# Weight sums of the seven-product units in another order, the first column released at the sixth product, and shared border transposes at the output

## Chip, cores and metric

The kernel runs on one core of a Trainium2 chip, in one launch. The metric is the device time of one execution in microseconds (us). Engines: PE is TensorE, with PEld its weight loads; DVE is VectorE, ACT ScalarE, POOL GpSimd and SP SyncE, which here mostly issues DMAs.

## What is computed

One streaming step of a hybrid layer for 512 prompt frames and 64 sample frames (576 frames, two halves of 288), all in fp32:

```python
hn = rmsnorm(x, g_norm1)
proj = hn @ w_in                                    # q, k, v | gb, gc, hc
q, k = rmsnorm(q, g_q), rmsnorm(k, g_k)
o_attn = stick_breaking_blocks(q, k_all, v_all, P)  # 8 heads x 128
u = gc * hc
conv = conv_w[0]*padded[:, 0:T] + conv_w[1]*padded[:, 1:T+1] + conv_w[2]*padded[:, 2:T+2]
o_conv = gb * conv                                  # 1024 channels
mix = concat([rmsnorm(o_attn, g_attn_out), rmsnorm(o_conv, g_conv_out)])
x = x + mix @ w_out
h2 = rmsnorm(x, g_norm2)
x = x + (silu(h2 @ w_gate) * (h2 @ w_up)) @ w_down
```

## The kernel before

An fp32 product is made of three fp32r matmuls: weights and frames are split into a high part (a CAST on ACT, then called the copy) and the rest (a TENSOR_TENSOR subtract on DVE, called the low part), and high x high, low x high and high x low are added up in PSUM.

Most large products are done in **units** of seven products in place of eight (Strassen-Winograd). A unit takes two weight columns of 128 (c = 0, 1), each cut by the parity of its input block: `a11`, `a12` lie in the first column, `a21`, `a22` in the second. The frames stand ready as 288-frame operands. Per unit four sums of 128 x 1024 weights are made on DVE. Before: at product 6 `s1 = a21 + a22`, `a21 = a21 - a11`, `a11 = s1 - a11`; at product 3 `a12 = a12 - a11`. Then products 1 to 7 use `a11, a12, a12', a22, s1, a11', a21'`. Products 1, 6, 5 and 3 add into one PSUM tile (`psy`), 7 and 4 into another (`psw`), 2 has its own (`psx`). ACT copies `psy` out (`part`) after products 1, 6 and 5, and DVE adds such parts to `psx` or `psw` (`cv`, in `done`).

The stages in order of time: attention heads and the first two convolution groups by plain products (line 214); `conv_run` (line 1012) with nine convolution units, numbers 0 to 8, and eight units 9 to 16 of the output projection's attention half, of 4 channel blocks in place of 8, whose frames (`forms`, seven of them, one per product) come back from DRAM; the other half of that projection by plain products; the first gate and up columns by plain products; gate and up units; down units (`run`, line 1526), whose results go out through `store_y` (line 1662).

For the convolution units, `corder` (line 1115) lists the products in their PE order as (unit, product). `conv_prepare` (line 968) makes the operand four places ahead: sums if due, the copy, the low part, into one of four `whl` buffers. PE's order is written out by hand. On ACT and DVE instructions stand in the order of the program only while `start_mode` is open (line 1128 on), else a scheduler places them; SP is in program order from unit 8 on (`turn_mode`).

Weight columns lie in three places: `raw_a` (two) and `raw_c`. `call_columns` (line 935) loads the next wanted column by an SP DMA as soon as one is free; a free place is announced by `conv_prepare`, the first column's at product 3, the second's at product 4. All SP DMAs go through one queue. At the start, columns (0,0), (0,1) and (1,0) (unit, column) are in place, and column (1,1) is the next. Just ahead of it SP issues the loads of the frame sums for products 4 and 5 of the convolution units: `xs_t` (line 862, 2304 KB) and eight loads of 288 KB into `x` (line 1112).

`store_y` turns a finished block of 128 columns x 288 frames by three PE transposes (128, 128 and 32 frames) into PSUM, copies 2 x 128 frames by one ACT copy and the 32 border frames by another (`obs`), and issues one DMA for the first half's 256 frames, three for the second half's, and one for each border. Each of eight down pairs d has four such blocks, (c, i) for column c and half i.

Of the kernel before, what the change touches and what calls it, by code (L numbers as in the profile page):

```python
# [20 lines left out]
HALF = T // 2  # L21
# [73 lines left out]
def tile_hybrid_stream_step(  # L95
# [6 lines left out]
    nc = tc.nc  # L102
# [119 lines left out]
    def split(hi, lo, src, lo_eng=None):  # L222
        nc.scalar.copy(out=hi, in_=src)  # L223
        (lo_eng or nc.vector).tensor_tensor(out=lo, in0=src, in1=hi.bitcast(F32), op=ALU.subtract)  # L224
# [259 lines left out]
    for i in range(5):  # L484
        n = P if i < 4 else TS
# [457 lines left out]
    def call_columns(gone):  # L943
        cfree.extend(gone)
        while cwanted:
            n, c = cwanted[0]
            place = [q for q in cfree if c is not None or q < 2][:1]
            if not place:
                return
            cwanted.pop(0)  # L950
            q = place[0]
            cfree.remove(q)
            raw = bt["raw"] if q == 2 else raw_tile["A"][:, q, :]
            if c is None:
                d = CU[n][1]
                nc.sync.dma_start(out=raw.rearrange("p (k c) -> p k c", c=2 * P),
                                  in_=w_out[:AW, 2 * d * P : 2 * (d + 1) * P].rearrange("(k p) c -> p k c", p=P))
                v = raw.rearrange("p (j s h c) -> p j s h c", s=2, h=2, c=P)
                for c in range(2):
                    cregion[n, c] = q, v[:, :, 0, c, :], v[:, :, 1, c, :]  # L960
            else:
                c0 = cstart[c + 2 * (CU[n][0] == "b")] + CU[n][1] * P
                nc.sync.dma_start(out=raw.rearrange("p (k c) -> p k c", c=P),
                                  in_=w_in[:, c0 : c0 + P].rearrange("(k p) c -> p k c", p=P))
                v = raw.rearrange("p (j s c) -> p j s c", s=2, c=P)
                cregion[n, c] = q, v[:, :, 0, :], v[:, :, 1, :]

    def conv_prepare(n, p_):
        st, tt, m = cst.setdefault(n, {"left": 7}), nc.vector.tensor_tensor, NP if n < NCU else NH // 2
        if p_ == 1:  # L970
            _, st["a11"], st["a12"] = cregion[n, 0]
        if p_ == 6:
            _, st["a21"], st["a22"] = cregion[n, 1]
            s1 = st["s1"] = bt["s1"][:, :m]
            tt(out=s1, in0=st["a21"], in1=st["a22"], op=ALU.add)
            tt(out=st["a21"], in0=st["a21"], in1=st["a11"], op=ALU.subtract)
            tt(out=st["a11"], in0=s1, in1=st["a11"], op=ALU.subtract)
        if p_ == 3:
            tt(out=st["a12"], in0=st["a12"], in1=st["a11"], op=ALU.subtract)
# [132 lines left out]
        nc.sync.dma_start(out=xt[j][:, 0, 1].bitcast(F32), in_=xs_dram[0, j].rearrange("f p t -> p f t"))  # L1112
    pipe.flush()
    open_units()
    corder = [(0, 1), (0, 2), (1, 1), (1, 2), (0, 6), (0, 7), (0, 5), (0, 3), (0, 4), (1, 6), (1, 7), (1, 5)]
    for n in range(2, len(CU)):
        if n == NCU - 1:
            corder += [(n, 1), (n - 1, 3), (n - 1, 4), (n, 6), (n, 7), (n, 5), (n, 2), (n, 4), (n, 3)]
        elif n == NCU:
            corder += [(n, 1), (n, 2), (n + 1, 1), (n + 1, 2), (n, 6), (n, 7), (n, 5), (n, 3), (n, 4)]  # L1120
            corder += [(n + 1, 6), (n + 1, 7), (n + 1, 5)]
        elif n == NCU + 1:
            pass
        else:
            corder += [(n, 1), (n - 1, 3), (n - 1, 4), (n, 2), (n, 6), (n, 7), (n, 5)]
# [478 lines left out]
    acc = {}  # L1604
    down = {}

    def take_blocks(d):

        if d in (0, 1, 3):
            spare_block({0: "z", 1: "t", 3: "ax"}[d])  # L1610
        if d in (0, 3):
            four = [down["z"][:, q, :] for q in (range(4) if d == 0 else range(4, 6))]
            if d:
                four += [down["ax"][:, q, :] for q in range(2)]
        elif d < 3:
            t = down["t"] if d == 1 else ypool.tile([P, 4, HALF], F32, tag=f"y{NP - 1}", name=f"acc{d}")
            four = [t[:, q, :] for q in range(4)]
        elif d < 6:
            four = [pool.tile([P, HALF], F32, tag=tag, name=f"acc{d}", bufs=2)
                    for pool, tag in (((tmp, "y"), (tmp, "r")) if d == 4 else ((tmp, "sq"), (h2pool, "hx")))  # L1620
                    for _ in range(2)]
        else:
            pool, tag = (tmp, "hl") if d == 6 else (rpool, "R")
            two = [pool.tile([P, 2, HALF], F32, tag=tag, name=f"acc{d}", bufs=2) for _ in range(2)]
            four = [t[:, q, :] for t in two for q in range(2)]
        for q, ap in enumerate(four):
            acc[d, q // 2, q % 2] = ap

    def spare_block(name):
        if name not in down:  # L1630
# [31 lines left out]
    def store_y(n, c, i):  # L1662

        d = UNITS[n][1]
        src, cs, f0 = acc[d, c, i], slice((2 * d + c) * P, (2 * d + c + 1) * P), HALVES[i][0]
        r = HALF - 2 * P

        def put(f, ap, q=nc.sync):

            rows, n_p = ap.shape[0], max(min(TP - f, ap.shape[0]), 0)  # L1670
            if n_p:
                q.dma_start(out=yp[f : f + n_p, cs], in_=ap[:n_p])
            if n_p < rows:
                q.dma_start(out=ys[f + n_p - TP : f + rows - TP, cs], in_=ap[n_p:])

        quick = n == NU - 1

        def work():
            yield 4 if quick else 9
            po = misc("pot")[:, : 3 * P]  # L1680
            for q in range(3):
                w = min(P, HALF - q * P)
                nc.tensor.transpose(po[:w, q * P : (q + 1) * P], src[:, q * P : q * P + w], ident)
            yield 0 if quick else 3
            ob = src[:, : 2 * P].rearrange("p (i c) -> p i c", c=P)
            nc.scalar.copy(out=ob, in_=po[:, : 2 * P].rearrange("p (i c) -> p i c", c=P))
            obs = down["pool"].tile([r, P], F32, tag="obs", name="obs", bufs=4)
            nc.scalar.copy(out=obs, in_=po[:r, 2 * P :])
            yield 0 if quick else 4
            if i == 0:  # L1690
                nc.sync.dma_start(out=yp[: 2 * P, cs].rearrange("(i p) c -> p i c", p=P), in_=ob)
            else:
                put(f0, ob[:, 0, :])
                put(f0 + P, ob[:, 1, :])
            put(f0 + 2 * P, obs, nc.scalar if quick else nc.sync)

        pipe.spawn(work())


# [76 lines left out]
```

## Time and profile before

| | us |
|---|---|
| three runs, median | 2407.14 (2403.85 to 2408.5) |
| the profiled execution, its time | 2407.74 |
| its span, first to last instruction | 2406.0 |

The same span by stages, from the windows of the profile (stage names are this text's):

| us from start | stage | PE busy | DVE busy | DMA share |
|---|---|---|---|---|
| 0 to 505 | heads, first two groups | 491.77 | 359.11 | 0.50 |
| 505 to 545 | start of the units | 33.28 | 29.95 | 0.73 |
| 545 to 714.5 | convolution units | 169.50 | 146.48 | 0.42 |
| 714.5 to 808.3 | output projection's units | 90.82 | 70.40 | 0.86 |
| 808.3 to 987 | plain products | 176.40 | 136.72 | 0.42 |
| 987 to 1895 | gate and up units | 908.00 | 758.48 | 0.47 |
| 1895 to 2406 | down units and stores | 503.83 | 397.52 | 0.60 |

Where PE is busy for a stage's whole length, only PE's own work sets its time; elsewhere the difference is idle PE, and the rows of waits say for whom. A row of a timeline has the start, the length, engine, line, operation, tiles, the count, and in brackets the idle time before it with what ended it.

### The profile page before, as it was taken

The page shows a single profiled execution, that of the slowest core. Times are in us where ns is not written, and L with a number is a line of the kernel's source. Part 1 is how long each engine was busy: PE and PEld are TensorE (multiplying, and loading weights), DVE is VectorE, ACT ScalarE, POOL GpSimd, SP SyncE. Part 2 cuts the span into 40 slices and gives each one's busy share as a digit, 9 for nine tenths or more (in the row PEclk, how much of TensorE's full clock was granted, in tenths as well). Part 3 has the DMA queues.
Part 4 walks back from the last instruction along what each step waited for, and adds up shares of the span by engine and source line. Part 5 has one row for each costly group of instructions (what it writes and reads, how often), then busy time and mean ns, then how long its engine had stood idle before and what let it go on. Part 6 is the DMA issues. An engine that isn't in the chain of part 4 may idle for free.

```text
span 2406.0 us, 44164 instructions
## 1 busy us (share of the span) xinstructions
PE 2373.6 (99%) x17825; PEld 2360.9 (98%) x17825; DVE 1898.7 (79%) x2854; ACT 1168.1 (49%) x2099; POOL 279.1 (12%) x384
## 2 busy tenths in 40 slices
PE   8999999989999999999999999999999999999999
PEld 8999999989999999999999999999999999999998
DVE  7767676678887768888888888888888777887875
ACT  6656565444444545444444444444444444444454
POOL 1111111231111120000000000000000001431211
PEclk9999999999999999999999999999999999999999
DMA  7354433584268733444444434534444945885642
GB/s 255 116 153 138 136 118 95 180 285 123 88 206 221 212 120 112 138 145 150 137 133 150 152 117 155 160 113 156 150 129 141 337 137 189 231 233 196 203 128 80
DMA packets 503956, 386.04 MB, mean 160 GB/s; under 512 B 11726, under 2 KB 492872, under 8 KB 503752
## 3 DMA queue, kind: packets, MB, share of 16 engines
q1 hardware_dynamic: 494408, 366.68, 47.8%
q0 software_dynamic: 8624, 16.22, 3.3%
q8 instruction: 139, 2.28, 0.4%
q14 instruction: 65, 0.53, 0.1%
q10 hardware_dynamic: 720, 0.33, 0.0%
HBM read 296.47 MB, written 86.72 MB: 159 GB/s over the span
## 4 chain that ended last, share of the span: by engine, by line
PE 88%; DVE 5%; DMA 3%; ACT 2%; issue 1%; SPq 1%; POOL 0%; ACTq 0%; POOLq 0%; DVEq 0%
PE psy L1526 33%; PE psw L1526 16%; PE pj L214 10%; PE psx L1526 8%; PE psy L1007 6%; PE pjo L214 4%; PE psw L1007 3%; PE pw L1369 2%; PE psx L1007 2%; DMA o_ob<-xt_dram 1%; DVE whl L224 1%; DMA forms<-form_dram 1%; DVE wlo L177 1%; PE z L685 0%; PE po L752 0%
## 5 line engine op out<-in xcount | busy, mean ns | idle before, releaser
L224 DVE TENSOR_TENSOR whl<-raw_a,whl 128x1024 fp32r<-128x1024 f32 (+4 forms) x372 | 391.0, 1051 | 76.4 <-ACT whl L223 74.9
L1526 PE MATMUL psy<-t,whl 128*128 128x288 f32 x2916 | 436.7, 295 | 0.0
L1526 PE MATMUL psy<-h_s,whl 128*128 128x288 f32 x2724 | 410.8, 295 | 1.7 <-ACT part L1536 1.7
L223 ACT CAST whl<-raw_a 128x1024 fp32r<-128x1024 f32 (+4 forms) x372 | 327.0, 881 | 163.9 <-issue 36.6
L1526 PEld LDWEIGHTS psy<-t,whl 128*128 128x128 f32 x2916 | 403.0, 188 | 0.2
L214 PE MATMUL pj<-x,whi 128*128 128x288 f32 x1856 | 398.4, 300 | 0.3 <-DVE x L357 0.3
L1526 PEld LDWEIGHTS psy<-h_s,whl 128*128 128x128 f32 x2724 | 377.4, 188 | 2.2 <-ACT part L1536 2.2
L1526 PE MATMUL psw<-t,whl 128*128 128x288 f32 x2592 | 376.9, 295 | 0.0
L1526 PEld LDWEIGHTS psw<-t,whl 128*128 128x128 f32 x2592 | 353.7, 188 | 0.2
L214 PEld LDWEIGHTS pj<-x,whi 128*128 128x128 f32 x1856 | 307.4, 189 | 1.0 <-DVE x L357 0.6
L214 PE MATMUL pj<-x,wlo 128*128 128x288 f32 x928 | 274.9, 296 | 0.1
L224 DVE TENSOR_TENSOR whl<-raw_b,whl 128x1024 fp32r<-128x1024 f32 (+5 forms) x186 | 194.0, 1043 | 70.1 <-ACT whl L223 69.1
L223 ACT CAST whl<-raw_b 128x1024 fp32r<-128x1024 f32 (+5 forms) x186 | 161.0, 868 | 161.8 <-issue 69.4
L1536 ACT COPY part<-psy 128x288 f32<-128x288 f32 x237 | 94.4, 398 | 267.5 <-PE psy L1526 266.4
L214 PEld LDWEIGHTS pj<-x,wlo 128*128 128x128 f32 x928 | 175.5, 189 | 0.7 <-DVE wlo L424 0.3
L1526 PE MATMUL psx<-h_s,whl 128*128 128x288 f32 x1122 | 164.6, 294 | 0.8 <-DVE gs L1349 0.8
L1526 PEld LDWEIGHTS psx<-h_s,whl 128*128 128x128 f32 x1122 | 154.0, 188 | 1.0 <-ACT form L223 1.0
L223 ACT CAST whl<-s 128x1024 fp32r<-128x1024 f32 (+5 forms) x79 | 70.1, 888 | 100.0 <-PE psw L1526 98.5
L1289 POOL DMA_DIRECT2D hid_dram<-form x3 | 2.2, 748 | 977.9 <-DVE form L224 976.0
L177 DVE TENSOR_TENSOR wlo<-raw_a,whi 128x1024 fp32r<-128x1024 f32 (+1 forms) x80 | 97.0, 1226 | 8.9 <-ACT whi L176 7.8
L214 PE MATMUL pjo<-mixc,whi 128*128 128x288 f32 x512 | 101.7, 294 | 0.0
L176 ACT CAST whi<-raw_a 128x1024 fp32r<-128x1024 f32 (+1 forms) x85 | 85.7, 1024 | 19.4 <-PE pjo L214 9.0
(449 smaller groups left out, 3959.5 us busy)
## 6 DMA issues: line engine op xcount, KB each, us to landing
hid_dram<-form SPq DMA_DIRECT2D x147, 288.0 KB, 2.4
raw_a<-in_w_in_dram SPq DMA_DIRECT2D x41, 1024.0 KB, 5.6
raw_a<-in_w_gate_dram SPq DMA_DIRECT2D x23, 1024.0 KB, 5.8
raw_a<-in_w_up_dram SPq DMA_DIRECT2D x23, 1024.0 KB, 5.4
raw_b<-in_w_gate_dram SPq DMA_DIRECT2D x21, 1024.0 KB, 6.6
raw_b<-in_w_up_dram SPq DMA_DIRECT2D x21, 1024.0 KB, 7.8
h_s<-hid_dram SPq DMA_DIRECT2D x10, 2016.0 KB, 9.7
raw_a<-in_w_out_dram SPq DMA_DIRECT2D x16, 1024.0 KB, 5.7
```

The lines of the kernel that those rows point to most:

```text
L176: nc.scalar.copy(out=hi[:, a:b], in_=raw[:, a:b])
L177: lo_eng.tensor_tensor(out=lo[:, a:b], in0=raw[:, a:b], in1=hi[:, a:b].bitcast(F32), op=ALU.subtract)
L214: mm(ps, w_[:, k, csl], x_, start=(k == 0 and n == 0), stop=(k == nk - 1 and n == 2))
L223: nc.scalar.copy(out=hi, in_=src)
L224: (lo_eng or nc.vector).tensor_tensor(out=lo, in0=src, in1=hi.bitcast(F32), op=ALU.subtract)
L1007: mm(ps, whl[:, w_, j, :], x_, start=(start and j == 0 and q == 0), stop=(j == m - 1 and q == 2), skip_group_check=True)
L1289: q.dma_start(out=hid_dram[fp][2 * n - 2 : 2 * n].rearrange("f p t -> p f t"), in_=t.bitcast(F32))
L1369: mm(pss[j, i], w_[:, k, j * P : (j + 1) * P], x_, start=(kk == 0 and k == 0 and n == 0), stop=(kk == 1 and k == 7 and n == 2))
L1526: mm(ps, whl[:, w_, j, :], x_, start=(start and j == 0 and q == 0), stop=(j == len(xs_) - 1 and q == 2), skip_group_check=True)
L1536: nc.scalar.copy(out=t, in_=st["y"])
```

## The change

1. `conv_prepare`: the four sums are made in another order and with other operands. At product 7 `a21 = a21 - a11` and `s2 = a21 + a22`, at product 6 `a21 = s2 + a11` and `s2 = a12 - s2`; `s2` lies in the tile that held `s1`. Copy and low part are written out (lines 983 and 986), the second sum of product 7 between them and both of product 6 behind them. Nothing is written into the first column any more.
2. The first column's place is announced when products 2 and 6 have been prepared, in place of product 3.
3. `corder` has 7 ahead of 6 in every unit. At the start, product (1, 2) is not prepared ahead of the loop: products (1, 2) and (0, 7) are prepared after (0, 2) has run, (0, 6) after (1, 1), (0, 5) and (0, 3) after (1, 2). `start_mode` lasts until (0, 5) has run, in place of (1, 2).
4. The loads of `forms` follow the new order: operands of 1 and 2 go where product 7's frames were, those of 7 and 6 where product 6's were; that of 4 is loaded ahead of 5 and 3 in place of after them.
5. `take_blocks` and `store_y`: for six of the eight pairs (not d = 4 and 5) the two halves lie side by side (`both`), and the 64 border frames between them are turned once, by the block of the pair that is stored second. The first one does two transposes, one ACT copy and no border DMA.

```diff
     def conv_prepare(n, p_):
...
-        if p_ == 6:
+        if p_ == 7:
             _, st["a21"], st["a22"] = cregion[n, 1]
-            s1 = st["s1"] = bt["s1"][:, :m]
-            tt(out=s1, in0=st["a21"], in1=st["a22"], op=ALU.add)
+            st["s2"] = bt["s1"][:, :m]
             tt(out=st["a21"], in0=st["a21"], in1=st["a11"], op=ALU.subtract)
-            tt(out=st["a11"], in0=s1, in1=st["a11"], op=ALU.subtract)
-        if p_ == 3:
-            tt(out=st["a12"], in0=st["a12"], in1=st["a11"], op=ALU.subtract)
-        src = st[{1: "a11", 2: "a12", 3: "a12", 4: "a22", 5: "s1", 6: "a11", 7: "a21"}[p_]]
+        src = st[{1: "a11", 2: "a12", 3: "s2", 4: "a22", 5: "a21", 6: "s2", 7: "a21"}[p_]]
...
-        split(whl[:, 0], whl[:, 1], src)
         coper[n, p_] = whl
-        if p_ in (3, 4):
-            q = cregion.pop((n, p_ - 3))[0]
-            if n < NCU or (n, 4 - p_) not in cregion:
-                call_columns([q])
+        nc.scalar.copy(out=whl[:, 0], in_=src)
+        if p_ == 7:
+            tt(out=st["s2"], in0=st["a21"], in1=st["a22"], op=ALU.add)
+        tt(out=whl[:, 1], in0=src, in1=whl[:, 0].bitcast(F32), op=ALU.subtract)
+        if p_ == 6:
+            tt(out=st["a21"], in0=st["s2"], in1=st["a11"], op=ALU.add)
+            tt(out=st["s2"], in0=st["a12"], in1=st["s2"], op=ALU.subtract)
+        if p_ in (2, 4, 6):
+            st["gone"] = st.get("gone", ()) + (p_,)
+            c = int(p_ == 4)
+            if c or (2 in st["gone"] and 6 in st["gone"]):
+                q = cregion.pop((n, c))[0]
+                if n < NCU or (n, 1 - c) not in cregion:
+                    call_columns([q])
...
-    corder = [(0, 1), (0, 2), (1, 1), (1, 2), (0, 6), (0, 7), (0, 5), (0, 3), (0, 4), (1, 6), (1, 7), (1, 5)]
+    corder = [(0, 1), (0, 2), (1, 1), (1, 2), (0, 7), (0, 6), (0, 5), (0, 3), (0, 4), (1, 7), (1, 6), (1, 5)]
...
-    for p_ in (1, 2):
-        conv_prepare(1, p_)
+    conv_prepare(1, 1)
...
-        if (n, p_) == (1, 2):
+        if (n, p_) == (0, 5):
             start_mode.close()
-        if k_ + 4 < len(corder):
-            conv_prepare(*corder[k_ + 4])
+        for q in ((), (3, 4), (5,), (6, 7))[k_] if k_ < 4 else range(k_ + 4, min(k_ + 5, len(corder))):
+            conv_prepare(*corder[q])
...
-            for at, f in enumerate({1: (1, 2), 2: (6, 7), 3: (5, 3)}[q]):
+            for at, f in enumerate({2: (1, 2), 1: (7, 6), 3: (5, 3)}[q]):
                 load_forms(t, 4 * at, f)
-            if p_ == 4:
+            if p_ == 6:
                 load_forms(apool.tile([P, NH // 2, 2, HALF], F32R, tag="oa", name="forms0"), 0, 4)
...
     def store_y(n, c, i):
...
+        lone = (d, c) not in both
+        k0 = 0 if lone or i == 0 else r
+        rest = None
+        if lone:
+            rest = src[:, 2 * P :], f0 + 2 * P
+        elif (d, c) in one:
+            rest = both[d, c].rearrange("p i t -> p (i t)")[:, 2 * P : 2 * P + 2 * r], 2 * P
+        one[d, c] = i
...
-            for q in range(3):
-                w = min(P, HALF - q * P)
-                nc.tensor.transpose(po[:w, q * P : (q + 1) * P], src[:, q * P : q * P + w], ident)
+            for q in range(2):
+                nc.tensor.transpose(po[:, q * P : (q + 1) * P], src[:, k0 + q * P : k0 + (q + 1) * P], ident)
+            if rest:
+                nr = rest[0].shape[1]
+                nc.tensor.transpose(po[:nr, 2 * P :], rest[0], ident)
```

More of the change, by code (lines that the diff above doesn't have):

```diff
@@ L1124, in tile_hybrid_stream_step @@
         else:
-            corder += [(n, 1), (n - 1, 3), (n - 1, 4), (n, 2), (n, 6), (n, 7), (n, 5)]
+            corder += [(n, 1), (n - 1, 3), (n - 1, 4), (n, 2), (n, 7), (n, 6), (n, 5)]
     corder += [(len(CU) - 1, 3), (len(CU) - 1, 4)]
@@ L1604, in tile_hybrid_stream_step @@
     acc = {}
+    both, one = {}, {}
     down = {}
@@ L1611, in take_blocks @@
         if d in (0, 3):
-            four = [down["z"][:, q, :] for q in (range(4) if d == 0 else range(4, 6))]
-            if d:
-                four += [down["ax"][:, q, :] for q in range(2)]
+            z = down["z"]
+            two = [z[:, 0:2, :], z[:, 2:4, :]] if d == 0 else [z[:, 4:6, :], down["ax"]]
         elif d < 3:
             t = down["t"] if d == 1 else ypool.tile([P, 4, HALF], F32, tag=f"y{NP - 1}", name=f"acc{d}")
-            four = [t[:, q, :] for q in range(4)]
+            two = [t[:, 0:2, :], t[:, 2:4, :]]
         elif d < 6:
@@ L1621, in take_blocks @@
                     for _ in range(2)]
+            for q, ap in enumerate(four):
+                acc[d, q // 2, q % 2] = ap
+            return
         else:
@@ L1624, in take_blocks @@
             two = [pool.tile([P, 2, HALF], F32, tag=tag, name=f"acc{d}", bufs=2) for _ in range(2)]
-            four = [t[:, q, :] for t in two for q in range(2)]
-        for q, ap in enumerate(four):
-            acc[d, q // 2, q % 2] = ap
+        for c, t in enumerate(two):
+            both[d, c] = t
+            for i in range(2):
+                acc[d, c, i] = t[:, i, :]
     def spare_block(name):
@@ L1680, in work @@
             po = misc("pot")[:, : 3 * P]
-            for q in range(3):
-                w = min(P, HALF - q * P)
-                nc.tensor.transpose(po[:w, q * P : (q + 1) * P], src[:, q * P : q * P + w], ident)
+            for q in range(2):
[3 more added lines that the diff above has]
+                nc.tensor.transpose(po[:nr, 2 * P :], rest[0], ident)
             yield 0 if quick else 3
-            ob = src[:, : 2 * P].rearrange("p (i c) -> p i c", c=P)
+            ob = src[:, k0 : k0 + 2 * P].rearrange("p (i c) -> p i c", c=P)
             nc.scalar.copy(out=ob, in_=po[:, : 2 * P].rearrange("p (i c) -> p i c", c=P))
-            obs = down["pool"].tile([r, P], F32, tag="obs", name="obs", bufs=4)
-            nc.scalar.copy(out=obs, in_=po[:r, 2 * P :])
+            if rest:
+                obs = down["pool"].tile([2 * r, P], F32, tag="obs", name="obs", bufs=4)
+                nc.scalar.copy(out=obs[:nr], in_=po[:nr, 2 * P :])
             yield 0 if quick else 4
@@ L1692, in work @@
             else:
-                put(f0, ob[:, 0, :])
-                put(f0 + P, ob[:, 1, :])
-            put(f0 + 2 * P, obs, nc.scalar if quick else nc.sync)
+                put(f0 + k0, ob[:, 0, :])
+                put(f0 + k0 + P, ob[:, 1, :])
+            if rest:
+                put(rest[1], obs[:nr], nc.scalar if quick else nc.sync)
         pipe.spawn(work())
```

6 lines of the change are left out of this document (3 added, 3 removed).

## The prediction

> **What bounds the kernel now.** I read the busy times first, then what PE waited for, then the timelines of the few places where it waited.
>
> ```profile
> PE 2373.6 (99%) x17825; PEld 2360.9 (98%) x17825; DVE 1898.7 (79%) x2854; ACT 1168.1 (49%) x2099; POOL 279.1 (12%) x384
> PE psx L1007 <- DVE cv L1031: 5.3, 1, 5.3
> PE psy L1007 <- ACT part L1016: 1.3, 2, 0.8
> PE psw L1007 <- DMA forms<-form_dram: 1.1, 1, 1.1
> PE psy L1007 <- ACT whl L223: 1.0, 1, 1.0
> PE psy L1007 <- DVE whl L224: 0.9, 1, 0.9
> 545.00:714.50 169.50, 169.50 (x1284) 169.50 (x1284) 146.48 (x195) 73.57 (x102) 23.48 (x45) 1.00 0.42 131
> ```
>
> PE is the bound: of a span of 2406.0 us it is idle for 32.4. The edit touches no matmul of a product, so it can win only idle PE, slow PE, or matmuls of the stores. In the products that it reorders (line 1007) PE waits 9.6 us in all. Between 545 and 714.5 it waits for nothing: columns released earlier, and sums dealt out otherwise, have nothing to win there. DVE, at 146.48 of 169.50, has about 14% to spare and gets the same number of sums, copies and low parts of the same shapes (1.22 us a sum and a low part, 1.05 a copy, in rows below); I cost it at nothing, with the rival below if that cover is gone. The released columns only move DMAs within a stage of 0.42 DMA share.
>
> **The start of the units, first as it is.**
>
> ```profile
> 512.56 3.34 PE L1007 MATMUL psy<-x,whl 128*128 128x288 f32 x23 [0.90 <-DVE whl L224]
> 521.24 5.56 PE L1007 MATMUL psx<-x,whl 128*128 128x288 f32 x24 [5.34 <-DVE cv L1031]
> 526.64 3.33 PE L1007 MATMUL psy<-xs_t,whl 128*128 128x288 f32 x24
> 529.81 3.33 PE L1007 MATMUL psw<-xs_t,whl 128*128 128x288 f32 x24
> 532.98 3.33 PE L1007 MATMUL psy<-x,whl 128*128 128x288 f32 x24
> 536.80 3.43 PE L1007 MATMUL psy<-x,whl 128*128 128x288 f32 x24 [0.49 <-ACT part L1016]
> 514.60 1.21 DVE L975 TENSOR_TENSOR cx<-raw_a 128x1024 f32<-128x1024 f32 x1
> 518.36 1.23 DVE L979 TENSOR_TENSOR raw_a<-raw_a 128x1024 f32<-128x1024 f32 x1
> 519.50 1.22 DVE L224 TENSOR_TENSOR whl<-raw_a,whl 128x1024 fp32r<-128x1024 f32 x1
> 520.64 0.45 DVE L1031 TENSOR_TENSOR cv<-psx,part 128x288 f32<-128x288 f32 x1
> ```
>
> Product (1, 2), the fourth, needs the PSUM tile that (0, 2) left; its evacuation `cv` stands on DVE behind unit 0's four sums (514.60 to 519.59) and a low part. So PE idles 5.34 us. Then its 24 matmuls take 5.56 us, where starts 3.17 apart (526.64, 529.81, 532.98) are the rule: 2.4 us more.
>
> The changed order has `cv` right behind DVE's `mx` and makes the sums later. Worked forward: (1, 1) still ends at 512.56 + 23 x 0.132 = 515.6; before that DVE does `cv`, one multiply and (1, 2)'s low part (ending about 515.4); sum, sum, and two low parts follow at 1.2 us each (about 518.9 and 520.1). So (1, 2) runs from 515.6, (0, 7) from 518.9, (0, 6) from 522.1, (0, 5) from 525.2. The fifth product starts 7.9 us before 526.8. That is the visible gain.
>
> **Where that gain goes.** Product (0, 3) adds onto the `psy` of (0, 5), so it waits for ACT to copy (0, 5)'s part: the 0.49 above. In the changed program ACT's instructions stand thus (its own line numbers):
>
> ```
> L1024 TensorCopy part_6333<-psy_6150
> L983 TensorCopy whl_6336<-raw_a_92
> L1024 TensorCopy part_6364<-psy_6150
> ```
>
> The third is (0, 5)'s part. Ahead of it, since `start_mode` now lasts to (0, 5), stands (1, 7)'s copy, which waits for a DVE sum and for column (1, 1)'s DMA. Before, that copy stood behind. Queued behind the waiting copy, and behind the sum on DVE, are the part, (0, 5)'s `cv` and so (0, 3) and (0, 4) on PE. The question is when the column lands.
>
> ```profile
> 515.21 7.22 SPq L1112 DMA_DIRECT2D x<-xs_dram  x6
> xs_t<-xs_dram SPq DMA_DIRECT2D x1, 2304.0 KB, 9.6
> x<-xs_dram SPq DMA_DIRECT2D x1, 288.0 KB, 9.9
> 528.00:529.00 1.00, 1.00 (x9) 1.00 (x9) 1.00 (x1) 0.00 (x0) 0.00 (x0) 1.00 0.34 121
> raw_a<-in_w_in_dram SPq DMA_DIRECT2D x1, 1024.0 KB, 5.6
> 532.00:533.00 1.00, 1.00 (x10) 1.00 (x9) 0.61 (x1) 0.00 (x0) 0.00 (x0) 1.00 1.15 348
> 534.84 1.23 DVE L975 TENSOR_TENSOR cx<-raw_a 128x1024 f32<-128x1024 f32 x1 [2.22 <-DMA raw_a<-in_w_in_dram]
> 536.10 1.23 DVE L976 TENSOR_TENSOR raw_a<-raw_a,raw_c 128x1024 f32<-128x1024 f32 x1
> 536.35 0.40 ACT L1016 COPY part<-psy 128x288 f32<-128x288 f32 x1 [5.00 <-PE psy L1007]
> 537.40 1.05 ACT L223 CAST whl<-raw_a 128x1024 fp32r<-128x1024 f32 x1 [0.65 <-DVE raw_a L976]
> ```
>
> The queue serves in order: a 288 KB load issued at 515.2 takes 9.9 us, landing just behind the 2304 KB ahead of it. It is full until 528.3 (0.34 of the slice from 528). The column can now be issued when unit 0's last sum ends, about 522.6, not at 529.2; but its 1.05 MB start at 528.3, take 3.0 us at 348 GB/s, and land about 0.6 later, as the last `x` load does (525.1 and five loads of 295 KB at 390 GB/s, 0.76 each, give 528.9): 531.8. Bounds: 531.0 (388 GB/s, no delay) to 532.5. From landing: sum to copy 1.30 (536.10 to 537.40), copy to the next ACT start 0.95, part to PE 0.45 (536.35 to 536.80), together 2.75 with 0.05 to begin. So (0, 3) starts at 534.5 (533.7 to 535.3), not 529; before, 536.8. The new stall is nearly as long as the old: (0, 5) must itself wait for the last `x` load at 528.9 and ends at 529.4, so PE idles 5.1 us. **Start: -2.3 us (-3.1 to -1.5).**
>
> What is late next is the clock.
>
> ```profile
> 518.00:519.00 1.00, 0.00 (x0) 0.00 (x0) 0.96 (x2) 0.58 (x1) 0.00 (x0) 1.00 1.05 369
> 519.00:520.00 1.00, 0.00 (x0) 0.00 (x0) 1.00 (x2) 1.00 (x2) 0.00 (x0) 0.58 1.07 396
> 525.00:526.00 1.00, 1.00 (x6) 1.00 (x6) 0.00 (x0) 0.00 (x0) 0.00 (x0) 0.50 1.09 388
> 526.00:527.00 1.00, 1.00 (x9) 1.00 (x9) 0.09 (x1) 0.17 (x1) 0.00 (x0) 1.00 1.09 389
> ```
>
> The granted clock fell to 0.50 at about 519.2, 3.3 us into the idle stretch, and stayed so to 526, 4.75 us after PE resumed. An idle stretch of 5.1 us is a little shorter than the 5.34 that did this. The three runs of before spread by 4.65 us, so such a loss need not come in every execution. I take half of 2.6 us (5.1 x half speed): **+1.3 us**, bounds 0 (idle ends before the fall) and +3.0. The Trainium skill ("TensorE: Matmul & The Clock Gate", What's actually happening) says that the gate counts activity in free-running windows of 3.4 us that are not tied to the kernel's start. The trace's 519.2 and 526.0 lie two such windows apart, which agrees. By the row alone 5.34 us went cold and 5.1 would too (+2.6); by the rule 5.1 us holds a whole window in (5.1 - 3.4) / 3.4, half of the executions, an estimate.
>
> **The output units' forms.**
>
> ```profile
> 724.59 1.75 PE L1007 MATMUL psy<-forms,whl 128*128 128x288 f32 x12
> 727.31 1.85 PE L1007 MATMUL psy<-forms,whl 128*128 128x288 f32 x12 [0.97 <-ACT whl L223]
> 730.30 1.83 PE L1007 MATMUL psw<-forms,whl 128*128 128x288 f32 x12 [1.14 <-DMA forms<-form_dram]
> 705.58 0.37 SPq L956 DMA_DIRECT2D raw_a<-in_w_out_dram  x1
> 707.00:708.00 1.00, 1.00 (x9) 1.00 (x9) 1.00 (x3) 0.00 (x0) 0.00 (x0) 1.00 0.74 188
> ```
>
> These are unit 9's products 5, 3 and 4; their operands are loaded in that order. That ACT row is misread: the part that 3 needs was done by 726.8, so it was form 3 that landed at 727.3, and form 4 at 730.2, 3 us each. The change loads 4 ahead of 5 and 3, though PE uses it last. Form 5 then lands in 3's slot and 3 in 4's. Against that, the column of 705.58 is released before the first forms and the next two loads no longer stand behind it, so the queue doesn't run low at 707: about 1.1 us sooner. Form 5 at 726.2, form 3 at 729.2, product 4 at 730.8 where it was 730.3: **+0.4 us**; with nothing gained +1.6, with 2.5 us gained -0.9. No idle stretch there reaches 3.3 us.
>
> ```profile
> 802.24 1.99 ACT L176 CAST whi<-raw_a 128x1024 fp32r<-128x1024 f32 x2 [0.67 <-PE psw L1007]
> 804.58 0.67 PE L1007 MATMUL psy<-forms,whl 128*128 128x288 f32 x3 [0.79 <-ACT part L1016]
> ```
>
> Unit 16's part of product 5 stands behind these two casts. With 6 after 7, the part of 6 comes 1.6 us later and starts the casts at about 802.5: **+0.3 us**.
>
> **The stores.**
>
> ```profile
> 2288.89 0.33 PE pot L1683 x3
> 2393.80 0.55 PE L1683 MATMUL pot<-ident,acc 128*128 128x128 f32 x3 [0.29 <-ACT obs L1688]
> ```
>
> Three transposes lengthen the chain, all PE there, by 0.33 us, 0.11 each. Six pairs d with two columns each lose one: 12 x 0.11 = **-1.3 us** (-0.9 if border ones are cheaper, -2.1 with waits for `obs` gone too). The 12 ACT copies, and 12 SP DMAs fewer, lie beside PE. The last block still does three transposes and four DMAs, so the tail keeps its length.
>
> **The sum.** 2407.74 - 2.3 + 1.3 + 0.4 + 0.3 - 1.3 = 2406.1 for the profiled execution, which stands 0.6 above the median 2407.14 of the runs: 2405.5. Low ends: -3.1 + 0 - 0.9 + 0.3 - 2.1 - 0.6 gives 2401.3; high ends: -1.5 + 3.0 + 1.6 + 0.3 - 0.9 gives 2410.2.
>
> **The rivals.** *The gain stays.* If the column landed by 526.7 (529.4 less 2.75), 4.1 us after its issue, or the part were copied first, the stall would go without a new one, but for 0.9 us for `x`: -7.0 in place of -2.3 + 1.3, so 2399.5. For it: the 6 us of DVE work in front of `cv` are truly gone. Against: 5.6 us even on an empty queue, this one full until 528.3, and the order on ACT.
>
> *The sum tile decides (slower).* It now holds `s2` from product 7 until product 3's low part, longer than `s1` until 5's, and the next unit's product 7 needs it. If DVE, 86% busy, ran late by more than its lead of two to three products, PE would wait once a unit; at 0.5 us for each of 16 units, +8: 2413.5. Against: the same amount of DVE work, and in the changed order the low part of product 3 stands ahead of the next unit's second sum by two products.
>
> *It does nothing at all*: the cold clock comes in full and the forms' early start is worth nothing: 2407.74 - 2.3 + 2.6 + 1.6 + 0.3 - 1.3 - 0.6 = 2408.0, inside the forecast's range.
>
> **How the numbers follow.** Forecast 0.76 (with the last case), the gain stays 0.13, the sum tile 0.11. A measurement of this kernel can tell about 0.2% (4.8 us) from no change. Of the forecast's 0.76 I put 0.06 below 2402.3 and 0.01 above 2412. So faster 0.19, same 0.69, slower 0.12. The range, 2400.3 to 2410.5, holds the forecast's ends and a part of the first rival.
>
> **What would show it.** Right: the wait for `cv` at the fourth product gone; a new one of about 5 us, for ACT's part, ahead of (0, 3) at about 534.5; (1, 7)'s copy just before that part, ended by the column's DMA; products 545 to 714.5 without idle PE; in the output units a wait at product 5 and at 3, none at 4; 84 transposes for 96. Wrong: (0, 3) near 529 (the gain stays), or many small waits of `psw` products for low parts (the sum tile).

## The result, and the profile after

The changed kernel takes 2416.78 us (median of 6 runs, 2414.14 to 2418.31); the kernel before, run beside it, 2407.53 (6 runs, 2403.47 to 2410.88). The ratio is 1.004 with a 95% interval of 1.0027 to 1.0053: slower by about 9 us, outside the range that was forecast. The profiled execution of the changed kernel is the fastest of its six, 2414.14 us with a span of 2412.4, so the two profiled spans lie only 6.4 us apart.

First the busy times and PE's waits of the changed kernel (waits: us in total, times, longest), then its window from 545 to 714.5 us (length; busy time and count of PE, PEld, DVE, ACT and POOL; granted clock; DMA share; GB/s). Line 1007 of the kernel before is line 1015 here.

```profile
PE 2376.9 (99%) x17813; PEld 2360.8 (98%) x17813; DVE 1899.6 (79%) x2854; ACT 1167.0 (48%) x2087; POOL 292.6 (12%) x384
...
PE psy L1015 <- ACT part L1024: 13.8, 19, 5.0
PE psy L1015 <- DMA forms<-form_dram: 1.2, 1, 1.2
PE psy L1015 <- DVE whl L986: 1.0, 1, 1.0
```

```profile
545.00:714.50 169.50, 165.60 (x1237) 163.75 (x1236) 141.03 (x184) 72.09 (x99) 33.18 (x43) 1.00 0.39 119
```

DVE's busy time is the same within 1 us, the wait for `cv` is gone, and one kind of wait has come: 19 times, 13.8 us in all, products on `psy` wait for ACT's `part`. PE, which had no idle time between 545 and 714.5, has 3.9 us of it there. One wait is the 5.0 at the start that the prediction describes; the other 18 take 8.8 us, 0.49 each: 17 of them stand ahead of a product 5, one in each unit, and the last ahead of (16, 3). One unit before, in PE's timeline (start, us, engine, line, operation, out<-in, tile, count, idle before it and its releaser):

```profile
559.12 3.33 PE L1007 MATMUL psw<-xs_t,whl 128*128 128x288 f32 x24
562.29 3.33 PE L1007 MATMUL psx<-x,whl 128*128 128x288 f32 x24
565.46 3.33 PE L1007 MATMUL psy<-xs_t,whl 128*128 128x288 f32 x24
568.63 3.33 PE L1007 MATMUL psw<-xs_t,whl 128*128 128x288 f32 x24
571.81 9.68 PE L1007 MATMUL psy<-x,whl 128*128 128x288 f32 x72
581.33 3.33 PE L1007 MATMUL psw<-xs_t,whl 128*128 128x288 f32 x24
```

The same unit in the changed kernel:

```profile
558.49 3.33 PE L1015 MATMUL psw<-xs_t,whl 128*128 128x288 f32 x24
561.67 3.33 PE L1015 MATMUL psx<-x,whl 128*128 128x288 f32 x24
564.84 3.33 PE L1015 MATMUL psw<-xs_t,whl 128*128 128x288 f32 x24
568.01 3.33 PE L1015 MATMUL psy<-xs_t,whl 128*128 128x288 f32 x24
571.84 9.81 PE L1015 MATMUL psy<-x,whl 128*128 128x288 f32 x72 [0.49 <-ACT part L1024]
581.49 3.33 PE L1015 MATMUL psw<-xs_t,whl 128*128 128x288 f32 x24
```

The rows of a unit are product 4 of the unit before, then 2, 6, 7 and 5 (the 72 matmuls are 5, then 1 and 3 of the neighbouring units); in the changed kernel 2, 7, 6, 5. Products 1, 6, 5 and 3 of a unit all add onto one `psy`, and behind 6 ACT copies it into the part `u2`. Before, 7 ran between 6 and 5 on another PSUM tile, and the copy lay beside its 3.17 us. Now 6 and 5 are neighbours, and 5 may not write `psy` until ACT has read it. From product 4 to product 4 the unit took 581.33 - 559.12 = 22.21 us and takes 581.49 - 558.49 = 23.00; a steady pair further on (604.48 and 627.47) gives 22.99. So 0.78 a unit, of which the profile lists 0.49 as idle. In the half-size output units it is the same: 739.90 to 751.00 before, 11.10, and 744.88 to 756.77 after, 11.89. Times 17 units: 13.3 us.

The start, in the changed kernel (PE, DVE and ACT), and the granted clock (third figure from the end):

```profile
520.97 3.33 PE L1015 MATMUL psy<-xs_t,whl 128*128 128x288 f32 x24
524.79 4.13 PE L1015 MATMUL psy<-x,whl 128*128 128x288 f32 x24 [0.49 <-ACT part L1024]
533.88 4.99 PE L1015 MATMUL psy<-x,whl 128*128 128x288 f32 x24 [4.96 <-ACT part L1024]
538.71 6.51 PE L1015 MATMUL psw<-xs_t,whl 128*128 128x288 f32 x48
531.18 1.23 DVE L978 TENSOR_TENSOR raw_a<-raw_a,raw_c 128x1024 f32<-128x1024 f32 x1 [5.55 <-DMA raw_a<-in_w_in_dram]
532.48 1.05 ACT L983 CAST whl<-raw_a 128x1024 fp32r<-128x1024 f32 x1 [7.75 <-DVE raw_a L978]
533.44 0.39 ACT L1024 COPY part<-psy 128x288 f32<-128x288 f32 x1
```

```profile
530.00:531.00 1.00, 0.00 (x0) 0.00 (x0) 0.00 (x0) 0.00 (x0) 0.00 (x0) 0.76 1.14 341
531.00:532.00 1.00, 0.00 (x0) 0.00 (x0) 0.82 (x1) 0.00 (x0) 0.00 (x0) 0.50 1.15 347
537.00:538.00 1.00, 1.00 (x8) 1.00 (x8) 0.80 (x1) 0.00 (x0) 0.00 (x0) 0.83 0.00 0
```

That part went as predicted: (0, 3) at 533.88 waits 4.96 for the part of (0, 5), which stands on ACT behind the copy of (1, 7), which waits for column (1, 1). The clock falls to 0.50 at about 530.5 and comes back at 537.4, so the 24 matmuls take 4.99 us.

The 6.4 us of span fall into three pieces. The stretch of the products, from the first product's start to the first matmul behind the last (line 214 on `mixc`), takes 808.40 - 505.02 = 303.38 us before and 818.03 - 503.56 = 314.47 after: +11.1. What lies ahead of it was 1.5 shorter in this execution, though the edit touches none of it but the last operands, and what lies behind it 3.2 shorter (2406.0 - 808.40 = 1597.6; 2412.4 - 818.03 = 1594.4). Of these 3.2, 2.1 lie ahead of the wait near 1914.40 (1921.92) that opens the last stage, in code that the edit does not touch.

### The profile page after: what moved, and what is told of

It reads as the page before. It is cut to its first block, busy times and chain, and to the rows that moved or that the text cites. A ratio compares the mean times of both kernels' runs of the same rounds, so it can differ in the third digit from the quotient of the medians.

```text
span 2412.4 us, 44103 instructions
## 1 busy us (share of the span) xinstructions
PE 2376.9 (99%) x17813; PEld 2360.8 (98%) x17813; DVE 1899.6 (79%) x2854; ACT 1167.0 (48%) x2087; POOL 292.6 (12%) x384
## 4 chain that ended last, share of the span: by engine, by line
PE 88%; DVE 4%; DMA 3%; ACT 2%; issue 1%; POOL 0%; SPq 0%; ACTq 0%; DVEq 0%; POOLq 0%
PE psy L1534 33%; PE psw L1534 16%; PE pj L214 11%; PE psx L1534 8%; PE psy L1015 6%; PE pjo L214 4%; PE psw L1015 3%; PE pw L1377 2%; PE psx L1015 1%; DMA o_ob<-xt_dram 1%; DVE wlo L177 1%; DMA forms<-form_dram 1%; DVE whl L224 1%; PE z L685 0%; DMA raw_a<-in_w_in_dram 0%
## 5 line engine op out<-in xcount | busy, mean ns | idle before, releaser
L224 DVE TENSOR_TENSOR whl<-raw_a,whl 128x1024 fp32r<-128x1024 f32 (+4 forms) x288 | 309.6, 1075 | 58.0 <-ACT whl L223 57.3
L223 ACT CAST whl<-raw_a 128x1024 fp32r<-128x1024 f32 (+4 forms) x288 | 259.4, 902 | 111.8 <-issue 35.4
L1015 PE MATMUL psy<-x,whl 128*128 128x288 f32 x648 | 91.4, 300 | 10.5 <-ACT part L1024 9.4
```

Of the source, the lines that this page charges most:

```text
L1015: mm(ps, whl[:, w_, j, :], x_, start=(start and j == 0 and q == 0), stop=(j == m - 1 and q == 2), skip_group_check=True)
```

## The experiments

Each was timed in five rounds beside the kernel before. Its medians there were 2406.85, 2407.51, 2406.84 and 2406.86, so the rows can be compared. "Stretch" is the stretch of the products in the profiled execution, as above; it leaves out what varies elsewhere.

| kernel | median, us | ratio to before, 95% interval | stretch, us |
| --- | --- | --- | --- |
| before | 2407.53 | | 303.4 |
| changed | 2416.78 | 1.0040 (1.0027 to 1.0053) | 314.5 |
| e1: before, order alone | 2420.58 | 1.0053 (1.0041 to 1.0066) | 316.5 |
| e2: changed, 6 ahead of 7 | 2412.80 | 1.0021 (1.0013 to 1.0030) | 310.9 |
| e3: changed, later (1, 7) | 2409.00 | 1.0008 (0.9999 to 1.0017) | 307.4 |
| e4: e2 and e3 | 2404.94 | 0.9990 (0.9981 to 0.9999) | 306.6 |
| e5: changed, 2 between | 2405.96 | 0.9996 (0.9987 to 1.0005) | 305.5 |
| e6: e5 and e3 | 2399.26 | 0.9966 (0.9953 to 0.9978) | 298.8 |
| e7: e6, form 4 last | 2399.03 | 0.9968 (0.9956 to 0.9980) | 298.4 |
| e8: e6, part in its own tile | 2399.22 | 0.9962 (0.9949 to 0.9974) | 296.3 |
| e9: before, start alone | 2405.02 | 0.9995 (0.9986 to 1.0004) | 303.9 |
| e10: before, stores alone | 2404.72 | 0.9990 (0.9982 to 0.9999) | 303.8 |
| e11: changed, 2 between, later (1, 7) | 2400.27 | 0.9970 (0.9958 to 0.9982) | 298.6 |

In e5 to e8 one product of unit 9 is made with a wrong operand (below), so what they give out is not the layer's result; they stand here for what their order of work costs.

**The order alone.** Everything of the kernel before is kept, but 7 runs ahead of 6; the old sums move to 7 with it, and the forms are loaded in the new order:

```
-        if p_ == 6:
+        if p_ == 7:
             _, st["a21"], st["a22"] = cregion[n, 1]
...
-            corder += [(n, 1), (n - 1, 3), (n - 1, 4), (n, 2), (n, 6), (n, 7), (n, 5)]
+            corder += [(n, 1), (n - 1, 3), (n - 1, 4), (n, 2), (n, 7), (n, 6), (n, 5)]
```

> The kernel before with one thing of the change: product 7 runs ahead of 6 in all 17 units (the old sums are made at 7, and the forms are loaded in the order 1, 2, 7, 6). Theory A, the neighbours: 6 and 5 add onto the same psy, and with 7 gone from between them 5 waits for ACT's copy of 6's part. Starts of like products in the changed kernel lie 22.99 us apart (558.49 to 581.49) where they lay 22.21 (559.12 to 581.33), so 0.78 us a unit, 13.3 for 17, of which the later stages gave back 2.1 in the profile of after: 2418 to 2421, with 17 waits of about 0.49 for the part at 5. Rival B, the new sums and the earlier columns are what costs: with the old sums there are no such waits, and the time stays at 2407.5 within 2.

Measured: 2420.58, and in PE's waits and one unit of its timeline:

```profile
PE psy L1007 <- ACT part L1016: 12.7, 20, 2.5
PE psx L1007 <- DVE cv L1031: 4.1, 1, 4.1
```

```profile
559.74 3.33 PE L1007 MATMUL psw<-xs_t,whl 128*128 128x288 f32 x24
573.08 9.81 PE L1007 MATMUL psy<-x,whl 128*128 128x288 f32 x72 [0.49 <-ACT part L1016]
582.73 3.33 PE L1007 MATMUL psw<-xs_t,whl 128*128 128x288 f32 x24
```

With the old sums, too, a unit takes 22.99 us (559.74 to 582.73). The stretch is 13.1 us longer than before, where 13.3 was worked out from the unit's period. That the two agree so well is in part luck: two of the 20 waits are longer than the rest (1.3 and 2.5 us) and add 2.9, while the start and the wait for the forms give about as much back. The order by itself, with the old sums, the old columns, the old start and the old stores, costs more than the whole change does. Theory A holds; theory B, by which this kernel would have stayed at 2407.5, falls.

**6 ahead of 7 again, new sums kept.** Operands are still made 7 first, and the loads of the forms follow the run order again:

```
+    porder = list(corder)
+    for k_ in range(len(corder) - 1):
+        n = corder[k_][0]
+        if n > 1 and corder[k_ : k_ + 2] == [(n, 7), (n, 6)]:
+            corder[k_ : k_ + 2] = [(n, 6), (n, 7)]
...
-            conv_prepare(*corder[q])
+            conv_prepare(*porder[q])
```

> The changed kernel with the products of units 2 to 16 run as 6, 7, 5 again; the operands are still made 7 ahead of 6 with the new sums, and the first column still goes at 6. Theory A: 15 units x 0.78 = 11.7 us go, less up to 2.1 that the later stages no longer give back: 2405 to 2407.5 (from 2416.8), units 22.2 and 11.1 us apart, no wait for a part at 5 from unit 2 on. Rival B: the cost is in the sums, so the waits stay or move to products 6 and 7: 2414 to 2418.

Measured: 2412.80, 4.0 below the changed kernel where 9 to 12 were expected. In the convolution units the theory holds (the product 4 rows stand at 559.71 and 581.92, 22.21 apart, without a wait). In the output units another wait came, shown here in PE's waits and in the timeline of PE and DVE:

```profile
PE psy L1015 <- ACT part L1024: 6.4, 4, 4.9
PE psy L1015 <- DVE whl L986: 4.7, 4, 1.7
PE psy L1015 <- DMA forms<-form_dram: 2.5, 2, 1.3
```

```profile
743.76 0.30 PE L1015 MATMUL psy<-forms,whl 128*128 128x288 f32 x1
744.44 0.69 DVE L978 TENSOR_TENSOR raw_a<-raw_a 128x512 f32<-128x512 f32 x1 [2.87 <-DMA raw_a<-in_w_out_dram]
745.05 0.68 DVE L986 TENSOR_TENSOR whl<-cx,whl 128x512 fp32r<-128x512 f32 x1
745.79 1.73 PE L1015 MATMUL psy<-forms,whl 128*128 128x288 f32 x11 [1.73 <-DVE whl L986]
```

Product 6 begins at 743.76, does the one matmul that needs the high part alone, and waits for its low part (745.05). That stands on DVE behind a difference that waited 2.87 us for a column. Running 6 a product earlier than its operand was made for takes 1.59 us of lead away, and in the output units, whose products are 1.59 us long, it evidently was no larger. Stretch: 3.6 us won instead of 11.7. Undoing the order on PE alone puts a DVE wait in the place of the ACT wait.

**The operand of (1, 7) behind the part of (0, 5).**

```
-        for q in ((), (3, 4), (5,), (6, 7))[k_] if k_ < 4 else range(...):
+        for q in ((), (3, 4), (5,), (6, 7), (8,), (), (9, 10))[k_] if k_ < 7 else range(...):
             conv_prepare(*corder[q])
+        if (n, p_) == (0, 5):
+            start_mode.close()
```

> The changed kernel with the operand of (1, 7) made behind the run of (0, 5), so that ACT's copy of the part of (0, 5) no longer stands behind the copy that waits for column (1, 1). Theory C, the order on ACT made the stall of 4.96 us ahead of (0, 3): it starts at about 529.4, when (0, 5) ends, the clock stays up, and 4.5 + 1.7 = 6.2 us go: 2410.6, bounds 2409 to 2412.5. Rival D, the column itself is too late, and the stall moves on to (1, 7): its operand is ready about 3.6 us behind the column's landing at 531.2, so 534.8, with PE there at 535.7; if it comes later than that by as much, PE waits there and the time stays at 2414 to 2417.

Measured: 2409.00, 7.8 below the changed kernel. The start of it:

```profile
521.31 3.83 PE L1015 MATMUL psy<-x,whl 128*128 128x288 f32 x24 [0.49 <-ACT part L1024]
525.63 3.48 PE L1015 MATMUL psy<-x,whl 128*128 128x288 f32 x24 [0.49 <-ACT part L1024]
```

```profile
525.18 0.40 ACT L1024 COPY part<-psy 128x288 f32<-128x288 f32 x1 [3.92 <-PE psy L1015]
528.78 1.05 ACT L983 CAST whl<-raw_a 128x1024 fp32r<-128x1024 f32 x1 [3.20 <-DVE raw_a L978]
```

From (0, 5) to (0, 3) it is 4.32 us where it was 9.09, the part is copied at 525.18, 3.6 us ahead of the copy of (1, 7), and the clock stays at 1.00. Theory C holds, at the edge of its bounds: the order on ACT made the stall, and the late column stalls nothing by itself. What remains at both rows is the neighbours' 0.49.

**Both.**

> The changed kernel with both edits: units 2 to 16 run as 6, 7, 5, and the operand of (1, 7) made behind the run of (0, 5). If A and C hold and add: 2406.3 - 6.2 = 2400, bounds 2397.5 to 2402, which is 5 to 10 below the kernel before. If either rival holds, 2405 to 2412.

Measured: 2404.94. It fell short of the 2400 for the reason e2 did (six waits for low parts, 4.5 us), and for one more: PE came to the forms earlier than they did.

```profile
720.46 3.17 PE L1015 MATMUL psy<-forms,whl 128*128 128x288 f32 x12 [3.72 <-DMA forms<-form_dram]
```

That is unit 9's product 5; its 12 matmuls take 3.17 us where 1.75 is the rule, at a clock of 0.50. In e6 below PE comes to the same product at 717.28, hardly later than here, and does not wait; the seven loads of the forms take 16.4 us on SP's queue there and 21.8 here. Why was not looked into.

**Product 2 between 6 and 5.** This keeps the operands' lead and hides the copy again:

```
-            corder += [(n, 1), (n - 1, 3), (n - 1, 4), (n, 2), (n, 7), (n, 6), (n, 5)]
+            corder += [(n, 1), (n - 1, 3), (n - 1, 4), (n, 7), (n, 6), (n, 2), (n, 5)]
```

> The changed kernel with product 2 between 6 and 5 from unit 2 on (order 7, 6, 2, 5; in units 9 and 10 the products of the two are laced: (9,7), (9,6), (10,2), (9,5), (10,7), (9,3), (10,6), (9,4), (10,5)). Operands are made four products ahead, as in the changed kernel, and the first column goes at 2. Theory A: any product that does not add onto psy hides ACT's copy of the part, as 7 did; here no operand is made later, so the waits for low parts that came up in the output units of the kernel with 6 ahead of 7 (1.73, 1.53, 1.25 us) do not come: 11.7 us go, 2405, bounds 2403 to 2407.5; units 22.2 and 11.1 us apart throughout. Rival B, the new sums and columns cost as well: waits for low parts or for columns stay in the output units and the time is 2409 to 2413, as with 6 ahead of 7.

> The kernel with product 2 between 6 and 5, and also with the operand of (1, 7) made behind the run of (0, 5), which alone took 7.8 us off the changed kernel. If the two add: 2397, bounds 2395 to 2400, some 10 below the kernel before. If the forms of the output units decide what comes early (in the kernel with both earlier edits product 5 of unit 9 waited 3.72 us for its form and then ran at half the clock), 2400 to 2404.

> The kernel with product 2 between 6 and 5 and the later operand of (1, 7), and with the form of product 4 loaded behind those of 5 and 3 again, as in the kernel before. If the early load of form 4 holds up form 5, then form 5 lands one load earlier, which is 3 us, the wait at product 5 of unit 9 shrinks by up to that, and 1 to 4 us go against the kernel without this edit. If the wait only moves on to product 4, the two are within 1 us.

> The kernel with product 2 between 6 and 5 and the later operand of (1, 7) once more, with one more line: the part of product 6 of unit 9 is kept in a tile of another tag, so that unit 10's part, which in the laced order is copied before (9, 4) has read unit 9's, does not fall on it. In the three kernels with the laced order before this one it did, and what (9, 4) added to was unit 10's part. The same instructions otherwise: 2399.3, bounds 2397.5 to 2401, some 8 below the kernel before; if the wait of 0.98 for a DVE sum or the 1.54 for a part in unit 10 came from that tile, up to 2 us less.

In these four, unit 9's product 3 is multiplied with an operand made from a sum of unit 10; all instructions are done, so the times can be read. Measured: 2405.96, 2399.26, 2399.03 and 2399.22. Putting 2 between takes 10.8 us off the changed kernel (8.9 of stretch), and the later operand of (1, 7) another 6.7. The convolution units are 22.2 us apart without a wait in units 2 to 7. Of the waits that are left behind the start, the longest stand at the seams (e6, from unit 8 and unit 10); another of 0.98 for a part is in unit 13:

```profile
701.16 3.44 PE L1015 MATMUL psw<-xs_t,whl 128*128 128x288 f32 x24 [0.98 <-DVE cv L1039]
...
726.91 5.07 PE L1015 MATMUL psy<-forms,whl 128*128 128x288 f32 x36 [1.54 <-ACT part L1024]
```

The order of form 4 makes no difference (e6 and e7 within 0.3 us): with 2 between, no product of unit 9 waits for a form in either. The part's own tile, e8, takes both waits for a part away in the profile: in place of the 1.54 there is 0.17 for a low part, and the one in unit 13 does not come. The stretch is 2.5 us shorter than e6's, but the medians, 2399.22 and 2399.26, do not show it. As the cause of the wrong operand, e8's expectation named the wrong tile. The one that the laced order writes too early is the tile of the sums, and the next order avoids that.

**The same in an order that the one sum tile allows.** Units 9 and 10 are laced only as far as (10, 2):

```
-            corder += [(n, 1), (n, 2), (n + 1, 1), (n + 1, 2), (n, 7), (n, 6), (n, 5), (n, 3), (n, 4)]
+            corder += [(n, 1), (n, 2), (n + 1, 1), (n, 7), (n, 6), (n + 1, 2), (n, 5), (n, 3), (n, 4)]
             corder += [(n + 1, 7), (n + 1, 6), (n + 1, 5)]
```

> Product 2 between 6 and 5 and the later operand of (1, 7), with units 9 and 10 no longer laced beyond (10, 2): (9,7), (9,6), (10,2), (9,5), (9,3), (9,4), (10,7), (10,6), (10,5). What was wrong in the laced order was the tile of the sums, of which there is one for all units: the operand of (10, 7) writes it ahead of the operand of (9, 3), which reads it; the tile of the part, which the last such kernel changed, was not the cause. In this order all operands of unit 9 are made ahead of unit 10's first sum. Two neighbours come back, (9, 5) to (9, 3) and (10, 6) to (10, 5), 0.78 each, for waits of 0.98 and 1.5 that the laced order had: 2399.5, bounds 2397.5 to 2402, some 7 below the kernel before and 17 below the changed one. If lacing itself was what gained: 2403 to 2406.

Measured: 2400.27, ratio 0.997 (0.9958 to 0.9982): 6.6 us below the kernel before and 16.5 below the changed one. Its waits:

```profile
PE psy L1015 <- ACT part L1024: 3.2, 6, 0.8
PE psy L1015 <- DVE whl L986: 1.4, 1, 1.4
PE psw L1015 <- DVE cv L1039: 1.0, 1, 1.0
```

Of 19 waits for a part six are left, where no product without `psy` was moved between. This version beats both kernels, the one before by 0.3%, and keeps all the rest of the change: the early column, the new sums and the new stores.

**The start alone, on the kernel before.** The start's list of operands as in e3, with the old sums, order and stores; in the old order it is the operand of (1, 6) that comes later.

> The kernel before with the start of the changed one alone: old sums, old order 6, 7, 5 and old stores, but the operands of the first units made in the order of the program, behind the evacuations, and that of (1, 6) behind the run of (0, 5). Theory E, the gain of the last kernels is in the order of DVE's and ACT's work at the start and not in the sums: the wait of 5.3 us for cv and the half clock (2.4) go; against that (0, 6) waits for three sums, a copy and a low part in a row, ready about 519.9 with PE there at 517.6: about 2.3 us stay. 2407.2 - 7.7 + 2.3 = 2402, bounds 2399 to 2404. Rival F, only the new sums can feed PE there: another wait takes the place of the first and the time stays within 2 of the kernel before.

Measured: 2405.02, and a stretch of 303.9, no shorter than the 303.4 of before.

```profile
PE psy L1007 <- DVE whl L224: 4.4, 5, 1.1
```

```profile
511.48 3.33 PE L1007 MATMUL psx<-x,whl 128*128 128x288 f32 x24
516.05 0.40 PE L1007 MATMUL psy<-xs_t,whl 128*128 128x288 f32 x1 [1.24 <-ACT whl L223]
517.32 4.86 PE L1007 MATMUL psy<-xs_t,whl 128*128 128x288 f32 x23 [0.86 <-DVE whl L224]
```

```profile
517.00:518.00 1.00, 0.69 (x5) 0.69 (x6) 0.98 (x2) 1.00 (x2) 0.00 (x0) 0.95 1.08 391
518.00:519.00 1.00, 1.00 (x6) 1.00 (x6) 0.96 (x3) 0.19 (x1) 0.00 (x0) 0.50 1.09 391
```

The wait for `cv` is gone, and (0, 4) starts 31.40 us after the first product (500.92 to 532.32) instead of 35.06. Against theory E, the half clock is not gone: after the two waits ahead of (0, 6) the clock falls to 0.50 at 517.9, and 23 matmuls take 4.86 us where about 3.3 is the rule. And the 3.7 us are given back: product 6 of three later units waits 1.08, 0.93 and 0.78 for its low part, which on DVE stands behind the unit's sums. Theory E holds for the place and fails in its sum, and rival F is nearer. That DVE with the old sums has no lead left to give is argued, not shown. The same start in e6 and e11 has one such wait at most, at the start, so what else differs there (the sums, the early column, the order) earns something; how much each of them does was not tried.

**The stores alone, on the kernel before** (the hunks from line 1602 on).

> The kernel before with the new stores alone (84 transposes for 96). The last stage, from the wait of 0.95 (0.96) at 1914.40 (1921.92) to the last transposes at 2400.89 (2407.45), took 486.49 us before and 485.53 in the changed kernel, 0.96 less. If that is the stores: -1, bounds -0.5 to -2, at the edge of what this many runs can tell. If the stores cost nothing or something and the 0.96 is of another source: 0 to +2.

Measured: 2404.72, ratio 0.999 (0.9982 to 0.9999), 2.1 us less with an interval from 0.2 to 4.3, so just beyond the bounds of -0.5 to -2. The profiled executions agree only in part. Behind the products, the three kernels with the old stores (before, e1, e9) took 1597.6, 1596.1 and 1597.4 us, and the ten with the new ones 1595.0 in the mean (1593.8 to 1597.4); but 0.8 of these 2.0 lie ahead of the last stage, in code that is the same in all. The last stage, measured as in the expectation, took 486.5 us in the three, 485.2 to 485.6 in seven of the ten, and 486.3 to 486.6 in e2, e7 and e10 itself. A gain near 1 us is likely; e10's own profile does not show it there.

## Why the prediction was wrong

**The step that failed** is the first: "The edit touches no matmul of a product, so it can win only idle PE, slow PE, or matmuls of the stores", and, of the stage between 545 and 714.5, "I cost it at nothing". Idle PE can also be made. The cost was put on DVE's budget (sums, copies and low parts of the same number), which held: DVE's busy time and the low parts are as before. It was not asked what each product had hidden. Product 7, on `psw`, was the cover of ACT's copy of 6's part, and the swap took it away in all 17 units. The prediction priced the swap in one place only, unit 16, at 0.3 us, as a part that "comes 1.6 us later". The price stood in its own fence, at 536.80: (0, 3) behind (0, 5) on the same `psy`, `[0.49 <-ACT part L1016]`, starting 3.82 us after its neighbour instead of 3.17. Seventeen times 0.78, 13.3 us, is missing from the sum; e1 shows it alone, with the same 22.99 us a unit.

**The start** was right in its mechanism and near in size. Forecast: a new stall of 5.1 us ahead of (0, 3), from a copy that waits for the column; measured 4.96, and e3 shows that the order on ACT is the cause. From the first product to (0, 4) it took 35.06 us before and 35.15 after; without unit 0's own 0.78 that is -0.7, where -2.3 + 1.3 = -1.0 was said. The column came about 0.8 later on the kernel's own clock than the 531.8 forecast.

**The clock** was taken as an even chance, half of 2.6. It fell in this stall, and the time lost in (0, 3) was 4.99 - 3.33 = 1.7 us.

**The forms** had the wrong sign: +0.4 was said; from unit 9's first product to the start behind (9, 4) it took 17.35 us before (714.61 to 731.96) and 16.71 after (719.45 to 736.16, the second half of the row at 734.57), with one neighbour's 0.78 in it, so -1.4. Why the forms came earlier, measured by PE's progress, stays open. Form 3 did keep PE waiting and product 4 no longer did, as said; but form 5 was on time.

```profile
729.87 1.82 PE L1015 MATMUL psy<-forms,whl 128*128 128x288 f32 x12 [0.55 <-ACT part L1024]
732.89 1.85 PE L1015 MATMUL psy<-forms,whl 128*128 128x288 f32 x12 [1.20 <-DMA forms<-form_dram]
734.57 3.34 PE L1015 MATMUL psw<-forms,whl 128*128 128x288 f32 x24
```

**The stores** at -1.3 lie inside what e10 measured, -2.1 (-4.3 to -0.2). In the profiles the last stage of the changed kernel is 0.96 shorter, that of e10 0.2.

With the missing term and the measured sizes of the others the sum of the stretch is -0.7 + 13.3 - 1.4 = 11.2, against 11.1 in the profile.

**The rivals.** "The sum tile decides" had the right side, the right number of places and nearly the right price (0.5 us in 16 units, 2413.5), but another mechanism: products on `psw` that wait for DVE's low parts. In the trace products on `psy` wait for ACT, and e1, where nothing of the sums has changed but the product that they are made at, pays in full. "The gain stays" did not happen, but its condition, the part copied first, is the edit of e3, which gave 7.8 us.

## What to carry to other kernels

Before two steps of an in-order engine are swapped, write down for each one what runs beside it: a step that shares no tile with its neighbours is often the cover of an evacuation, and the order costs one release and refill wherever two accumulations into the same PSUM tile, between which that tile has to be copied out, become neighbours (0.78 us here). A stage without idle time on the bound engine has nothing to win from a new order, but each hidden wait in it to lose. And when such a cover must move, move another independent step into its place; running the old order with operands made for the new one only moves the wait to the engine that makes them.

## What the runs showed of the hardware

**The profile's idle time understates a short release.** Each wait for the part is listed as 0.49 us and costs 0.78: the product starts 0.65 late (571.84 - 568.01 = 3.83, where 3.17 is the rule), and its row of 72 matmuls takes 9.81 us instead of 9.68.

**The clock fell in every long wait between 505 and 725 us, in some sooner than 3.4 us after the last matmul.** Seven stalls of 3.72 to 5.34 us in these runs (before, after, e1, e2, e4, e5, e10) all brought it to 0.50. In the changed kernel (0, 5) ended at 528.9 and the clock fell at 530.5, 1.6 us later; in e1 it was 2.1, in e2 2.3, in the kernel before 3.3, and 3.7 to 4.1 in the other three. It then stayed down for 6.8 us (530.5 to 537.3). In e9 no single wait was longer than 1.24 us there, and it fell all the same: PE idled 1.24 and 0.86 us with one matmul between, the clock fell at 517.9, 0.6 us after PE ran again, and stayed down for 3.4 us. The Trainium skill ("TensorE: Matmul & The Clock Gate", What's actually happening) gives the cold state "after ≥1 idle window (~3.4µs)". The 6.8 us of the changed kernel and the 3.4 of e9 agree with the length of two windows and of one; the fall after 1.6 us of idleness, and that of e9, do not agree with a window that must be wholly idle. The prediction's even chance rested on that reading.

**Executions differ ahead of the edit by up to 5.8 us.** The first product started between 500.76 us (e3) and 506.52 (e8) in kernels whose first 500 us differ in nothing but the last operands. Comparing the stretch that an edit touches, as in the table, separates what two spans mix.
